# First loads on three queues, memory chunks scaled on two engines, the last row stored in four pieces, and another instruction order

## Chip, cores and metric

One core of a Trainium2 chip runs the kernel as one launch. Its engines are TensorE (PE, matrix products; PEld is its loading of weights), VectorE (DVE), ScalarE (ACT), GpSimd (POOL) and SyncE (SP). SP, ACT and POOL issue DMA transfers, each on a queue of its own. The metric is the device time of one execution in microseconds (us), as the median of several runs.

## What is computed

A decoder block over 512 positions of width 1024 (D), with 256 memory tokens, four heads of 256, and a feed-forward width of 2816:

```python
h = rmsnorm(x); proj = h @ w_in                      # 9216 columns
p_a, p_b, q, p_g = split(proj)
y_a = (gb * causal_conv3(gc * v)) @ w_a_out          # gb, gc, v from p_a
y_b = silu(layernorm(causal_conv31(u * sigmoid(ug)) + bias)) @ w_b_out
k, vm = split((rmsnorm(mem) * norm_mem_g) @ w_kv)
y_c = attention(q, k, vm) @ w_att_out
x = x + (g0 * y_a + g1 * y_b + g2 * y_c) @ w_o       # g = sigmoid(p_g + b_gate)
u = causal_conv3(rmsnorm(x) @ w_up); gt, up = split(u)
x = x + (silu(gt) * up) @ w_down
return rmsnorm(x) * norm_final_g
```

Inputs, weights and output are 32-bit floats.

## The kernel before

**Products.** A 32-bit matrix is split into a high part (rounded to the type that PE multiplies fast) and a low part (the rest). `product` (L632 to L636) makes three matmuls of each: high times high, high times low, low times high. ACT forms the high part of a weight block by a cast (`whi`, L683), DVE the low part by a subtraction (`wlo`, L687). Weights arrive in blocks of 512 KB (128 x 1024).

**Quads.** The big projections are cut into quads of 512 output channels, multiplied with seven products in place of eight: products 1 to 7 of a quad use sums and differences of blocks of the weights and of the activations (`ft4` to `ft7`, `fb00`, `fb10`, `fb11`). Sums of weights are made by adding transfers on POOL's queue (L808) or on DVE. One product is `multiply` (L866): 24 matmuls with 256 columns. Several products share a PSUM bank, and between them somebody must read the bank: product 4 may start only when DVE has read product 7's result with `minus` (L640, tile `uu`), products 6 and 7 after reads by ACT, and so on. A first matmul of a product is written with another access pattern of the same data (128x2x8x16 in place of 128x256) where the table `FRESH` names it.

**The order.** The kernel describes its work as jobs, each with an engine, a cost, the jobs it follows and the buffers it takes. A planner (`Jobs`) works out a due time for each from the order on PE and sets every engine's order. Three tables move its choices: `LATER` shifts due times, `AHEAD` tells how early a job may be issued, and `MOVES` edits the order on PE. The instructions are then written to the program in this order, so each engine runs through a fixed list.

**The start.** PE runs 11 warm-up products (`warm_up`, L2105) on a constant. SP loads the first half of the memory (`mem`, L947), then K's first weights (`ld0 K`, L1081), then V's; ACT's queue loads the gains (`pk`, 128 x 16, L628). When both are there ACT scales the four chunks of the memory by their gains (`mg`, L954), and PE multiplies the keys' first tile straight from these (K0, L1146), in two halves that wait for two chunks each. ACT then makes the memory's high part (`mh`, L966), DVE its low part (`ml`, L977), for the products after it.

**The end.** The output has four row tiles (t = 0 to 3) of 128 positions. For the last one DVE adds the two last banks (L2429), ACT sums squares (L2432) and takes the root (L2453), DVE the reciprocal (L2501). Then DVE scales the left 512 columns (`left_scaled`, L2463) and ACT the right ones (`right_scaled`, L2459), and SP and ACT each store a half (`stored`, L2468).

Of the kernel before, what the change touches and what calls it, by code (L numbers as in the profile page):

```python
# [8 lines left out]
F32 = mybir.dt.float32  # L9
F32R = mybir.dt.float32r  # L10
AF = mybir.ActivationFunctionType
# [3 lines left out]
P = 128  # L15
# [62 lines left out]
    "ACT c3": -190.4, "ACT cf": 13.1, "ACT csq": 651, "ACT exp": -246.7, "ACT fh h b00": -1,  # L78
# [4 lines left out]
    "ACT mg0": 6, "ACT mgh a": 11.9, "ACT mgh b": -6, "ACT mgh c": -22.7, "ACT mgh d": -539,  # L83
    "ACT mgh e": -123, "ACT mgh g": 4, "ACT mh": 472, "ACT mu high": 22, "ACT oh": -68.6,
    "ACT pth": -80, "ACT qh": -60.7, "ACT r1 bb": 75, "ACT r1 cv": 61.8, "ACT r1 gate": 335.4,
# [5 lines left out]
    "ACT sc": -95, "ACT sg": -4.8, "ACT sigmoid": 49, "ACT silu": 91, "ACT sq": -65, "ACT sr": -14,  # L91
    "ACT st": -0.2, "ACT swish": -944, "ACT tap 0": 323, "ACT tap 1": 95, "ACT tap 2": 5,
# [8 lines left out]
    "ACT xg": 33.2, "ACT xroot": -347, "ACT xsquare": 120, "ACT zh a": -186, "ACT zh b": -50,  # L101
    "ACT zh c": -3.4, "ACT zh e": -11, "ACT zh f": -93, "ACT zh g": -0.8, "DVE CV": 16.7,
    "DVE c3": -233, "DVE centre": 100, "DVE cf": 121.1, "DVE csum": -12, "DVE ends": -93.7,
# [6 lines left out]
    "DVE lns": -4.6, "DVE low": -427, "DVE m scale": -18, "DVE mfold": 2, "DVE mfold2": 277,  # L110
    "DVE mgl a": -2.1, "DVE mgl b": -5, "DVE mgl c": -11, "DVE mgl d": 400.7, "DVE mgl g": -334.1,
    "DVE ml": 82, "DVE ms c": -232, "DVE ms e": -2.2, "DVE ms f": 266, "DVE msum": -7,
    "DVE mu fold": -70, "DVE mu low": -150, "DVE mu sum": -187, "DVE ol": 10.7, "DVE pn": -22.2,
# [7 lines left out]
    "DVE sum": 167.8, "DVE tap 0": 898, "DVE tap 1": 336, "DVE tap 2": 0.8, "DVE tap 3": 567,  # L121
    "DVE top": -3576.1, "DVE tot1": 143.2, "DVE tot2": -268.9, "DVE v scale": 78.8,
    "DVE var fold": 114, "DVE var sum": 8, "DVE vl": -9.8, "DVE weigh": -226, "DVE wl K 0": 89.1,
# [8 lines left out]
    "DVE xn": 12.6, "DVE xnorm": -40, "DVE xsum": 40.6, "DVE y t4": -169, "DVE y t5": -5,  # L132
# [9 lines left out]
    "POOL wadd x": -1269, "POOL wadd y": 4, "POOL wl merge 0": 3.3, "POOL wl merge 2": -163.8,  # L142
# [372 lines left out]
def hybrid_block_kernel(  # L515
# [429 lines left out]
    for g in range(2):  # L945
# [1639 lines left out]
```

## Time and profile before

| what | value |
|---|---|
| runs, without the profiler | 918.60, 918.65, 918.81 us; median 918.65 us |
| profiled execution, its own time | 918.8 us |
| its span, first to last instruction | 917.0 us |
| granted TensorE clock, mean | 0.999 of full speed |
| PE busy / DVE / ACT / POOL | 908.5 / 848.7 / 684.6 / 137.1 us |
| transfers | 196.91 MB, mean 215 GB/s |

In a list of waits a row names the waiting engine, its tile and line, then the engine that ended the wait, and after the colon the total in us, the number of waits and the longest one. A row of the timeline has the start in us, the duration, the engine, the line, the operation, the tile it writes and those it reads, a count, and in brackets the idle time ahead of it with what ended it. SPq and ACTq are transfers as issued by these engines. A row that ends in KB and a number tells the median time in us from a transfer's issue to its landing. A row of the stretches has the window, its length, and for each engine its busy time and instructions, then PE's clock, the transfers' share and their GB/s; with one engine asked for, only that one.

### The profile page before, as it was taken

What the parts mean: (1) busy time and instruction counts of PE and PEld (TensorE: products, weight loads), DVE (VectorE), ACT (ScalarE), POOL (GpSimd) and SP (SyncE); (2) the same over time, 40 slices, a digit from 0 to 9 for tenths busy, and PEclk for the clock granted to TensorE, in tenths of its full rate; (3) what the DMA queues carried; (4) which work ended last, traced back from release to release, by engine and by line L of the source; (5) the groups of instructions that cost most, each with busy time, mean ns of one, the idle gap of its engine ahead of it and who ended that gap; (6) DMA issues with size and microseconds to landing.
All of it is one profiled execution on the core that took longest, in us unless ns stands there. A gap on an engine that the chain in (4) does not pass through costs nothing.

```text
span 917.0 us, 17020 instructions
## 1 busy us (share of the span) xinstructions
PE 908.5 (99%) x6789; PEld 858.7 (94%) x6789; DVE 848.7 (93%) x965; ACT 684.6 (75%) x940; POOL 137.1 (15%) x164
## 2 busy tenths in 40 slices
PE   9999999999999999999999999999999999999997
PEld 8999999999989999999899997899999999988886
DVE  6996999999999999999898989898979899999977
ACT  7777978889988876879748874767757676765566
POOL 0021111101011121110111211121211111002210
PEclk9999999999999999999999999999999999999999
DMA  9999778746769799786958999999999687779962
GB/s 367 371 293 196 153 177 201 157 117 150 212 144 274 167 197 239 151 185 176 227 126 242 204 260 322 260 219 293 276 259 215 143 194 161 191 258 316 270 136 93
DMA packets 55377, 196.91 MB, mean 215 GB/s; under 512 B 6273, under 2 KB 6401, under 8 KB 55297
## 3 DMA queue, kind: packets, MB, share of 16 engines
q0 software_dynamic: 22608, 81.54, 49.4%
q1 hardware_dynamic: 32400, 114.02, 34.3%
q8 instruction: 53, 0.87, 0.4%
q10 hardware_dynamic: 288, 0.27, 0.1%
q14 instruction: 28, 0.22, 0.1%
HBM read 191.60 MB, written 4.19 MB: 214 GB/s over the span
## 4 chain that ended last, share of the span: by engine, by line
PE 99%; DVE 1%; issue 0%; ACT 0%; DVEq 0%
PE bank L866 65%; PE bank L634 7%; PE bank L636 7%; PE bank L635 7%; PE bank L1705 3%; PE bank L1706 3%; PE bank L1704 3%; PE bank L1157 2%; PE bank L1938 1%; PE bank L2105 1%; PE bank L1146 0%; PE bank L1400 0%; PE bank L1993 0%; PE ss L1021 0%; DVE z L2073 0%
## 5 line engine op out<-in xcount | busy, mean ns | idle before, releaser
L683 ACT CAST whi<-wf 128x1024 fp32r<-128x1024 f32 (+1 forms) x197 | 205.2, 1044 | 96.4 <-PE bank L866 48.7
L687 DVE TENSOR_TENSOR wlo<-wf,whi 128x1024 fp32r<-128x1024 f32 (+1 forms) x191 | 230.0, 1213 | 12.3 <-ACT whi L683 12.0
L1472 ACT ACTIVATE tp<-u,pk 128x511 f32<-128x511 f32 (+22 forms) x184 | 119.0, 705 | 6.9 <-DVE acc L1479 5.8
L1479 DVE TENSOR_TENSOR acc<-acc,tp 128x1022 f32<-128x1022 f32 (+22 forms) x92 | 109.4, 1191 | 8.4 <-ACT tp L1472 6.8
L808 POOL DMA_DIRECT2D wf<-in_w_in x43 | 39.4, 938 | 217.0 <-DVE wlo L687 187.2
L866 PE MATMUL bank<-ft4h,whi 128*128 128x256 f32 x248 | 68.6, 277 | 0.9 <-DVE uu L640 0.9
L866 PE MATMUL bank<-fb10h,whi 128*128 128x256 f32 x248 | 68.7, 277 | 0.0
L866 PE MATMUL bank<-fb00h,whi 128*128 128x256 f32 x248 | 68.7, 277 | 0.0
L866 PE MATMUL bank<-ft7h,whi 128*128 128x256 f32 x248 | 68.7, 277 | 0.0
L866 PE MATMUL bank<-ft5l,whi 128*128 128x256 f32 x248 | 68.7, 277 | 0.0
L866 PE MATMUL bank<-fb11h,whi 128*128 128x256 f32 x248 | 68.7, 277 | 0.0
L866 PE MATMUL bank<-ft6l,whi 128*128 128x256 f32 x248 | 68.6, 277 | 0.0
L866 PE MATMUL bank<-ft6h,whi 128*128 128x256 f32 x248 | 68.6, 277 | 0.0
L866 PE MATMUL bank<-ft6h,wlo 128*128 128x256 f32 x248 | 68.6, 276 | 0.0
L866 PE MATMUL bank<-ft7l,whi 128*128 128x256 f32 x248 | 68.6, 276 | 0.0
L866 PE MATMUL bank<-ft5h,whi 128*128 128x256 f32 x248 | 68.6, 276 | 0.0
L866 PE MATMUL bank<-ft5h,wlo 128*128 128x256 f32 x248 | 68.5, 276 | 0.0
L866 PE MATMUL bank<-ft7h,wlo 128*128 128x256 f32 x248 | 68.5, 276 | 0.0
L866 PE MATMUL bank<-fb10l,whi 128*128 128x256 f32 x248 | 68.5, 276 | 0.0
L866 PE MATMUL bank<-fb10h,wlo 128*128 128x256 f32 x248 | 68.5, 276 | 0.0
L866 PE MATMUL bank<-ft4l,whi 128*128 128x256 f32 x248 | 68.5, 276 | 0.0
L866 PE MATMUL bank<-fb00l,whi 128*128 128x256 f32 x248 | 68.5, 276 | 0.0
(418 smaller groups left out, 3172.1 us busy)
## 6 DMA issues: line engine op xcount, KB each, us to landing
wf<-in_w_in SPq DMA_DIRECT2D x50, 512.0 KB, 5.9
wf<-in_w_in POOLq DMA_DIRECT2D x43, 512.0 KB, 6.6
wf<-in_w_up SPq DMA_DIRECT2D x31, 512.0 KB, 6.9
wf<-in_w_up POOLq DMA_DIRECT2D x30, 512.0 KB, 7.2
wf<-in_w_down SPq DMA_DIRECT2D x15, 512.0 KB, 6.1
wf<-in_w_kv SPq DMA_DIRECT2D x8, 512.0 KB, 8.7
wf<-in_w_v SPq DMA_DIRECT2D x8, 512.0 KB, 8.1
wf<-in_w_att_out SPq DMA_DIRECT2D x8, 512.0 KB, 4.1
```

Of the source, the lines that this page charges most:

```text
L634: nc.tensor.matmul(ps, s_hi, w_hi, start=start, stop=False, skip_group_check=again)
L635: nc.tensor.matmul(ps, s_hi, w_lo, start=False, stop=False, skip_group_check=again)
L636: nc.tensor.matmul(ps, s_lo, w_hi, start=False, stop=stop, skip_group_check=again)
L683: nc.scalar.copy(parts[0], src())
L687: nc.vector.tensor_tensor(lo, src(), hi.bitcast(F32), op=ALU.subtract)
L808: nc.gpsimd.dma_start(out=tiles[key], in_=block(w, col[c], k), accum_op=ALU.add)
L866: nc.tensor.matmul(to, w[:, k, at], col, start=first and n == 0, stop=k == 3 and n == 2, skip_group_check=again,)
L1472: nc.scalar.activation(two(("tp", p, s))[:, j, s:], two(("u", p))[:, j, : SEQ - s], AF.Copy, scale=weight(j),)
L1479: nc.vector.tensor_tensor(a, a, two(("tp", p, s))[:, :, s:], op=ALU.add)
L1704: nc.tensor.matmul(ps, w_hi[:, i, at], hi, start=first, stop=False)
L1705: nc.tensor.matmul(ps, w_hi[:, i, at], lo, start=False, stop=False)
L1706: nc.tensor.matmul(ps, w_lo[:, i, at], hi, start=False, stop=last)
```

## The change

Five edits:

1. The load of the gains goes to POOL's queue, ahead of POOL's first work; the constant `mean_w` is made by DVE in place of ACT.
2. K's first weights are loaded from ACT's queue in place of SP's.
3. The four memory chunks are scaled on ACT (chunks 0 and 2) and DVE (1 and 3) in place of ACT alone, as four jobs.
4. Both halves of the last row are scaled in two pieces of 256 columns (`ENDS`), and each piece is stored by itself: the left two from SP, the right first one from POOL, the right second one from ACT.
5. `LATER`, `AHEAD`, `FRESH` and some of `MOVES` have other entries.

```diff
 LATER = {
-    "ACT c3": -190.4, "ACT cf": 13.1, "ACT csq": 651, "ACT exp": -246.7, "ACT fh h b00": -1,
...
+    "ACT cf": 470, "ACT exp": -1067.2, "ACT fh h b00": -451, "ACT fh h b10": -0.1,
...
 FRESH = {
-    (("glu", 2), 7), (("q", 1), 5), (("bb", 0), 7), (("bb", 1), 1), (("gate", 0, 1), 2),
-    (("up", 2), 1), (("up", 0), 5), (("up", 0), 4), (("up", 1), 4), (("up", 2), 6),
+    (("glu", 2), 7), (("q", 1), 5), (("q", 1), 7), (("cv", 0), 7), (("cv", 2), 1), (("bb", 1), 2),
+    (("gate", 0, 0), 4), (("mq", 1), 3), (("up", 0), 5), (("up", 0), 6), (("up", 0), 4),
+    (("up", 1), 7), (("up", 1), 4), (("up", 2), 6),
 }
 MOVES = [
...
-    ((("up", 1), 7), (("up", 1), 4)),
-    ((("up", 1), 2), (("up", 0), 5)),
-    (("tr", 0), ("tr", 1)),
+    (("tr", 2), ("tr", 3)),
+    (("tr", 0), ("wo", "g", 0, 1)),
...
 AHEAD = {
...
+    pk = const.tile([P, N_PACKED], F32, tag="pk", name="pk")
+    nc.gpsimd.dma_start(out=pk[:, :N_GAINS], in_=packed[:, :N_GAINS])
     make_identity(nc, ident)
...
     nc.vector.memset(mean_col, 1.0 / D)
+    nc.vector.tensor_copy(mean_w, mean_col.broadcast_to([P, P]))
     nc.scalar.preload_act_table_set("sqrt_and_others")
-    nc.scalar.dma_start(out=pk[:, :N_GAINS], in_=packed[:, :N_GAINS])
-    nc.scalar.copy(mean_w, mean_col.broadcast_to([P, P]))
...
-            def mem_scaled(e=e):
-                if e == 0:
-                    make(("mg0",))
-                for i in range(2 * e, 2 * e + 2):
-                    nc.scalar.activation(
-                        four(("mg0",))[:, i, :], four(("mem", 0))[:, i, :], AF.Copy,
-                        scale=par("norm_mem_g", i),
-                    )
+            def mem_scaled(i):
+                to, t, scale = four(("mg0",))[:, i, :], four(("mem", 0))[:, i, :], par("norm_mem_g", i)
+                if i % 2:
+                    nc.vector.tensor_scalar(to, t, scale, None, op0=ALU.mult)
+                else:
+                    nc.scalar.activation(to, t, AF.Copy, scale=scale)
...
-        job(("ld0", s), "SP", LOAD, lambda: nc.sync.dma_start(out=tiles[raw], in_=src),
-            [("raw tile", s)], LOAD_LATENCY, use=[raw])
+        job(("ld0", s), "SP", LOAD, lambda: (nc.scalar if s == "K" else nc.sync).dma_start(
+            out=tiles[raw], in_=src), [("raw tile", s)], LOAD_LATENCY, use=[raw])
...
-                   lambda e=e: keys_product(0, 0, (2 * e, 2 * e + 1)), [("ld0", "K"), ("mg0", e)],
+                   lambda e=e: keys_product(0, 0, (2 * e, 2 * e + 1)), [("ld0", "K"), ("mg0", 2 * e), ("mg0", 2 * e + 1)],
...
+        for e, part in enumerate(ENDS if t == last else (slice(0, SEQ),)):
+            job(("sl", t, e), "DVE", 0.37 if t == last else 0.67,
+                lambda t=t, part=part: left_scaled(t, part), [("rc", t)])
+            job(("st", t, 0, e), "SP", STORE, lambda t=t, part=part: stored(t, 0, nc.sync, part),
+                [("sl", t, e)], LOAD_LATENCY)
+        for e, part in enumerate(ENDS if t == last else (slice(0, SEQ),)):
+            job(("sc", t, e), "ACT", 0.4 if t == last else 0.62,
+                lambda t=t, part=part: right_scaled(t, part),
+                [("rc", t), ("hd", t)] + ([("sc", t, 0)] if e else []))
+            queue, on, cost = ("SP", nc.sync, STORE)
+            if t == last:
+                queue, on, cost = (("ACT", nc.scalar, 0.4) if e else ("POOL", nc.gpsimd, 0.9))
+            job(("st", t, 1, e), queue, cost, lambda t=t, part=part, on=on: stored(t, 1, on, part),
+                [("sc", t, e)], LOAD_LATENCY)
```

**The order at the start.** ACT's first rows (each row: line, operation, the tile written and those read, its size) before, and in the changed program. `wf` with `in_w_kv` is K's first weights, `whi` the high part of V's.

```order
L627 ACT_TABLE_LOAD
L628 DMA pk<-in_packed 128x16
L629 CAST mean_w<-mean_col 128x128
L954 ACTIVATE mg_8_118<-mem_95,pk 128x256 x4
L966 CAST mh_129<-mg_8_118 128x512 x2
L1091 CAST whi_141<-wf_97 128x512 x2
```

```order
L626 ACT_TABLE_LOAD
L1080 DMA wf_96<-in_w_kv 128x1024
L952 ACTIVATE mg_6_112<-mem_95,pk 128x256 x2
L961 CAST mh_123<-mg_6_112 128x512 x2
L1090 CAST whi_141<-wf_97 128x512 x2
```

ACT now issues K's load in place of the gains, and scales two chunks in place of four; SP's list goes from `mem` straight to V's first weights.

**The order around product 7 of quad up 1.** PE before and after. `bank_6975` before and `bank_6959` after are the same bank of that quad; `ft7` and `ft4` are the operands of its products 7 and 4, `ft5` that of product 5 of quad up 2 (`bank_7414`).

```order
L866 MATMUL bank_6975<-ft7h_7101,whi_7333 128x256
L866 MATMUL bank_6975<-ft7l_7102,whi_7333 128x256
L866 MATMUL bank_6975<-ft7h_7101,wlo_7334 128x256
L866 MATMUL bank_6975<-ft4h_7207,whi_7372 128x2x8x16
L866 MATMUL bank_6975<-ft4l_7208,whi_7372 128x256
```

```order
L863 MATMUL bank_6959<-ft7h_7101,whi_7300 128x256
L863 MATMUL bank_6959<-ft7l_7102,whi_7300 128x256
L863 MATMUL bank_6959<-ft7h_7101,wlo_7301 128x256
L863 MATMUL bank_7414<-ft5h_7067,whi_7334 128x256
L863 MATMUL bank_7414<-ft5l_7068,whi_7334 128x256
L863 MATMUL bank_7414<-ft5h_7067,wlo_7335 128x256
```

Before, product 4 follows product 7 of its quad directly; now the 24 matmuls of product 5 of the next quad stand between them.

**The order at the end.** ACT's last rows before, and in the changed program. `x_1236` is the last row tile, `j` the squares' scratch, `cols` the sums.

```order
L2459 ACTIVATE x_1235_9730<-x_1235_9730,cols 128x512
L2432 ACTIVATE j_9646,cols<-x_1236_9731 128x256 x2
L2453 ACTIVATE cols<-cols 128x1
L2459 ACTIVATE x_1236_9731<-x_1236_9731,cols 128x512
L2468 DMA out<-x_1236_9731 128x512
```

```order
L2458 ACTIVATE x_1235_9729<-x_1235_9729,cols 128x512
L2431 ACTIVATE j_9646,cols<-x_1236_9730 128x256 x2
L2452 ACTIVATE cols<-cols 128x1
L2458 ACTIVATE x_1236_9730<-x_1236_9730,cols 128x256 x2
L2467 DMA out<-x_1236_9730 128x256
```

The scaling is now two instructions, and ACT stores one quarter of the row; POOL's list now ends with such a store too, and SP's with two.

More of the change, by code (lines that the diff above doesn't have):

```diff
@@ new lines @@
+    "ACT fh y t7": -2.4, "ACT high": -4.2, "ACT kh": 6.5, "ACT m root": -60, "ACT mg0": -13,
+    "ACT mgh a": 624, "ACT mgh b": -3, "ACT mgh c": 139.8, "ACT mgh d": 224.7, "ACT mgh g": 231,
+    "ACT mh": 238, "ACT msq": -372.8, "ACT mu high": 79, "ACT pth": -99.7, "ACT r1 bb": -395.5,
[6 rows of a table added]
+    "ACT sigmoid": -2.6, "ACT silu": -186, "ACT sq": -48, "ACT sr": -39, "ACT st": -158,
+    "ACT swish": -889.5, "ACT tap 0": 10.9, "ACT tap 1": 196.2, "ACT tap 2": -200.5,
[9 rows of a table added]
+    "ACT xg": 33.4, "ACT xroot": -141, "ACT xsq": 3.3, "ACT xsquare": -21, "ACT zh a": -322,
@@ new lines @@
+    "ACT zh b": -124.5, "ACT zh c": 17, "ACT zh d": 156, "ACT zh e": 118.3, "ACT zh g": 15.1,
+    "DVE CV": 8.9, "DVE c3": -2535, "DVE centre": 11.5, "DVE cf": 383, "DVE csum": -3,
[6 rows of a table added]
+    "DVE kt": 361.5, "DVE lns": -3.2, "DVE low": -120, "DVE m scale": 194, "DVE mfold": 187,
+    "DVE mfold2": -359.7, "DVE mgl a": 35, "DVE mgl b": 3.6, "DVE mgl c": -235.7, "DVE mgl d": 26.2,
+    "DVE mgl e": -35.6, "DVE mgl g": -1.4, "DVE ml": 3, "DVE ms c": -181.7, "DVE ms d": -47.9,
+    "DVE ms f": -1138, "DVE msum": 836, "DVE mu fold": -484, "DVE mu low": -59.2, "DVE mu sum": 208,
@@ new lines @@
+    "DVE ol": -602, "DVE pn": -694, "DVE ptl": -2738, "DVE ql": -793, "DVE r2 bb": -27,
[6 rows of a table added]
+    "DVE sum": 661.9, "DVE tap 0": 163, "DVE tap 2": -31.6, "DVE tap 3": 1414.3, "DVE top": -2751.7,
+    "DVE tot1": 118, "DVE tot2": 107, "DVE um": 329.9, "DVE v scale": -8, "DVE var sum": -40,
[8 rows of a table added]
+    "DVE x1 g": -263, "DVE xfold": -58.6, "DVE xn": -10, "DVE xnorm": -138.3, "DVE y t4": 79.5,
[8 rows of a table added]
+    "POOL s7 gate": -102, "POOL s7 glu": -189, "POOL s7 up": -73, "POOL wadd e": -208,
+    "POOL wadd x": -280, "POOL wadd y": 2.8, "POOL wl merge 0": -113, "POOL wl merge 2": 4.1,
[6 rows of a table added]
@@ L173 @@
     ((("up", 5), 7), (("up", 7), 1)),
[L174 to L186 removed]
+    ((("up", 5), 6), (("up", 7), 5)),
+    ((("up", 4), 3), (("up", 5), 6)),
+    ((("up", 4), 4), (("up", 4), 3)),
+    ((("up", 5), 2), (("up", 4), 4)),
+    ((("up", 3), 3), (("up", 6), 1)),
+    ((("up", 4), 7), (("up", 6), 5)),
+    ((("up", 3), 4), (("up", 4), 7)),
+    ((("up", 4), 6), (("up", 5), 1)),
+    ((("up", 3), 7), (("up", 4), 6)),
+    ((("up", 3), 6), (("up", 4), 2)),
+    (("tr", 2), ("tr", 3)),
+    (("tr", 0), ("wo", "g", 0, 1)),
     ((("mq", 1), 2), (("mq", 1), 6)),
@@ L236 @@
 AHEAD = {
[3 rows of a table removed]
-    "ACT high": 10, "ACT kh": 20, "ACT m root": 5, "ACT mgh c": 10, "ACT mgh d": 40,
-    "ACT mgh g": 10, "ACT mh": 5, "ACT oh": 2, "ACT pth": 20, "ACT qh": 2, "ACT r1 bb": 80,
[4 rows of a table removed]
-    "ACT swish": 150, "ACT tap 3": 80, "ACT tp 3": 150, "ACT v root": 150, "ACT vh": 80,
[4 rows of a table removed]
-    "ACT xsq": 80, "ACT xsquare": 150, "ACT zh a": 80, "ACT zh b": 40, "ACT zh c": 10,
[3 rows of a table removed]
-    "DVE h2 t4": 40, "DVE hd": 40, "DVE low": 150, "DVE m scale": 10, "DVE mfold": 20,
-    "DVE mgl a": 10, "DVE mgl b": 5, "DVE mgl c": 150, "DVE mgl e": 40, "DVE ml": 150,
-    "DVE ms d": 20, "DVE ms e": 10, "DVE msum": 150, "DVE mu fold": 2, "DVE mu low": 2,
-    "DVE mu sum": 20, "DVE ol": 10, "DVE pn": 5, "DVE ptl": 10, "DVE ql": 40, "DVE r2 bb": 20,
[4 rows of a table removed]
-    "DVE sl": 20, "DVE tap 2": 150, "DVE top": 20, "DVE tot1": 150, "DVE tot2": 10,
-    "DVE var sum": 20, "DVE vl": 10, "DVE wl K 0": 150, "DVE wl merge 2": 5, "DVE wl mix 3": 5,
[9 rows of a table removed]
-    "POOL wadd x": 20, "POOL wadd y": 40, "POOL wl merge 0": 10, "POOL wl merge 2": 2,
[4 rows of a table removed]
+    "ACT csq": 10, "ACT fh h b10": 5, "ACT fh h t4": 150, "ACT fh h t5": 20, "ACT fh h t6": 20,
+    "ACT fh h t7": 80, "ACT fh h2 t4": 10, "ACT fh h2 t5": 150, "ACT fh h2 t7": 150,
+    "ACT fh y b00": 10, "ACT high": 5, "ACT kh": 20, "ACT m root": 20, "ACT mg0": 20,
+    "ACT mgh b": 5, "ACT mgh e": 20, "ACT msq": 20, "ACT oh": 10, "ACT pth": 150, "ACT r1 bb": 40,
[3 rows of a table added]
+    "ACT st": 150, "ACT swish": 80, "ACT tap 3": 40, "ACT tp 2": 150, "ACT tp 3": 150,
[4 rows of a table added]
+    "ACT wn merge 2": 40, "ACT wn wo 0": 80, "ACT x root": 5, "ACT xg": 40, "ACT xroot": 5,
+    "ACT xsq": 80, "ACT xsquare": 10, "ACT zh c": 150, "ACT zh e": 150, "ACT zh f": 40,
+    "ACT zh g": 20, "DVE CV": 150, "DVE c3": 10, "DVE centre": 20, "DVE csum": 40,
[3 rows of a table added]
+    "DVE low": 40, "DVE mfold2": 5, "DVE mgl a": 80, "DVE mgl b": 10, "DVE mgl c": 2,
+    "DVE mgl d": 40, "DVE mgl e": 150, "DVE mgl g": 2, "DVE ml": 20, "DVE ms c": 2, "DVE ms d": 150,
+    "DVE ms e": 10, "DVE ms f": 150, "DVE mu low": 10, "DVE ol": 2, "DVE pn": 2, "DVE ptl": 150,
[4 rows of a table added]
+    "DVE top": 10, "DVE tot1": 150, "DVE tot2": 150, "DVE v scale": 20, "DVE var fold": 20,
[4 rows of a table added]
+    "DVE x1 d": 80, "DVE x1 e": 2, "DVE x1 f": 150, "DVE xfold": 80, "DVE xsum": 2, "DVE ymul": 40,
[8 rows of a table added]
 }
@@ L990, in hybrid_block_kernel @@
             if g == 0:
-                job(("mg0", e), "ACT", 2 * scaled_act(256), mem_scaled,
-                    [("mg0", 0) if e else ("ldm", 0, 0)],
-                    take=[] if e else [(source, ANY)], use=[("mem", 0)] + ([source] if e else []))
-            ready = ([] if e else [("ldm", 1, 0)]) if g else [("mg0", e)]
+                if e == 0:
+                    job(("mg0 tile", 0), "NONE", 0.0, lambda: make(("mg0",)), [("mem tile", 0)],
+                        take=[(source, ANY)])
+                for i in (2 * e, 2 * e + 1):
+                    job(("mg0", i), "DVE" if i % 2 else "ACT", 0.36 if i % 2 else scaled_act(256),
+                        lambda i=i: mem_scaled(i), [("ldm", 0, 0), ("mg0 tile", 0)],
+                        use=[("mem", 0), source])
+            ready = ([] if e else [("ldm", 1, 0)]) if g else [("mg0", 2 * e), ("mg0", 2 * e + 1)]
             job(("mh", g, e), "ACT", 2 * scaled_act(256) if g else actv(512), mem_high,
@@ L2127, in hybrid_block_kernel @@
         for side in sides
-    } | {("mg0", e) for e in range(2)}
+    } | {("mg0", i) for i in range(4)}
     GLU = [("glu", p) for p in range(4)]
@@ L2455, in root, with right_scaled, left_scaled, stored @@
         )
-    def right_scaled(t):
-        x1 = late["x1"][t][1]
+    def right_scaled(t, cols=slice(0, SEQ)):
+        x1 = late["x1"][t][1][:, cols]
         nc.scalar.activation(x1, x1, AF.Copy, scale=r_fin[t])
-    def left_scaled(t):
-        x1 = late["x1"][t][0]
+    def left_scaled(t, cols=slice(0, SEQ)):
+        x1 = late["x1"][t][0][:, cols]
         nc.vector.scalar_tensor_tensor(
-            x1, x1, r_fin[t], late["g"][0], op0=ALU.mult, op1=ALU.mult
+            x1, x1, r_fin[t], late["g"][0][:, cols], op0=ALU.mult, op1=ALU.mult
         )
-    def stored(t, i, queue):
+    def stored(t, i, queue, cols=slice(0, SEQ)):
         queue.dma_start(
-            out=out[t * P : (t + 1) * P, i * 512 : (i + 1) * 512], in_=late["x1"][t][i]
+            out=out[t * P : (t + 1) * P, i * 512 + cols.start : i * 512 + cols.stop],
+            in_=late["x1"][t][i][:, cols],
         )
```

38 lines of the change are left out of this document (1 added, 37 removed), and 162 rows, old and new, of tables (AHEAD, LATER).

## The prediction

> **What bounds the kernel now.** I read the page's first part, then the chain of waits, then what TensorE (PE) waits for, then the span cut into stretches.
>
> ```profile
> span 917.0 us, 17020 instructions
> PE 908.5 (99%) x6789; PEld 858.7 (94%) x6789; DVE 848.7 (93%) x965; ACT 684.6 (75%) x940; POOL 137.1 (15%) x164
> PE 99%; DVE 1%; issue 0%; ACT 0%; DVEq 0%
> PE bank L2105 <- DVE mean_col L626: 0.9, 1, 0.9
> PE bank L866 <- DVE uu L640: 0.9, 1, 0.9
> PE bank L636 <- DVE zl L2274: 0.4, 1, 0.4
> 6.00:300.00 294.00, 294.00 (x2230) 280.00 (x2230) 276.60 (x321) 247.16 (x366) 40.00 (x46) 1.00 0.82 217
> 910.70:917.00 6.30, 0.00 (x0) 0.00 (x0) 1.41 (x4) 1.52 (x4) 0.00 (x0) 0.82 0.57 218
> ```
>
> PE is busy 908.5 of 917.0 us. The chain agrees, and the list of PE's waits (total, count, mean) says how little there is to win inside: 0.9 at the start, one wait of 0.9 for the vector engine's (DVE's) `uu`, one of 0.4 for its `zl`. The stretch 6 to 300 us has PE busy 294.00 of 294.00, and the last 6.30 us hold no matmul. As the change leaves every product in place, it can touch four things only: when the first real product starts, the waits in the middle, waits that the new order makes, and the tail. What lies outside the span is 918.8 − 917.0 = 1.8 us and I leave it alone. The profiled 918.8 is 0.15 over the median 918.65, to which I add the sum.
>
> **The start.** Rows of the queues and engines in order of time, then issue to landing:
>
> ```profile
> 0.74 0.39 SPq L947 DMA_DIRECT2D mem<-in_mem_t  x1
> 1.19 0.42 SPq L1081 DMA_DIRECT2D wf<-in_w_kv  x1
> 1.66 0.42 SPq L1081 DMA_DIRECT2D wf<-in_w_v  x1
> 0.77 0.39 ACTq L628 DMA_DIRECT2D pk<-in_packed  x1
> mem<-in_mem_t SPq DMA_DIRECT2D x1, 512.0 KB, 3.9
> wf<-in_w_kv SPq DMA_DIRECT2D x1, 512.0 KB, 4.7
> pk<-in_packed ACTq DMA_DIRECT2D x1, 8.0 KB, 4.0
> 4.90 1.71 ACT L954 ACTIVATE mg<-mem,pk 128x256 f32<-128x256 f32 x4 [2.57 <-DMA pk<-in_packed]
> 0.93 5.06 PE L2105 MATMUL bank<-mean_col 128*128 128x128 f32 x22 [0.93 <-DVE mean_col L626]
> 5.98 4.08 PE L1146 MATMUL bank<-mg,wf 128*128 128x256 f32 x16
> ```
>
> Landings: mem 0.74 + 3.9 = 4.64, pk 0.77 + 4.0 = 4.77, K's weights 1.19 + 4.7 = 5.89. The scaling starts at 4.90, 0.13 after pk. The first K product starts at 5.98, when three things have come together: the weights (5.89), two scaled chunks (4.90 + 1.71 / 2 = 5.76), and PE itself, whose warm-up runs to 0.93 + 5.06 = 5.99. The warm-up is not changed, so an earlier landing or a faster scaling wins nothing here: the lower bound of this term is 0. This is the first expected gain that is hidden anyway.
>
> What can be lost: K's load now leaves ACT's queue beside mem's on SP, instead of behind it. That queues share the engines is seen in pk: 8 KB took 4.0 us beside a load of 512 KB that took 3.9. Two loads of 512 KB issued together should then end together, at the time when both were in before, 5.89. Then the chunks start at 5.89 + 0.13 = 6.02. A pair, one chunk on ACT beside one on DVE, takes 1.71 / 4 = 0.43, and 0.1 more to the product: 6.6 instead of 5.98, **+0.6**.
>
> A rule speaks against this part. The Trainium skill, DMA: Bandwidth & Descriptors, section "Rules for kernel authors", says that spreading loads over SP, ACT and GpSimd brings no bandwidth, because all run on the same 16 engines and interleave; it saves issue time only. The trace agrees with its 4.0 beside 3.9. By this rule the term is a loss or nothing, never a gain.
>
> The other price is pk on POOL's queue, whose first load it is. Nearest rows, POOL quiet and POOL's first load of the old order, beside a lone load on SP and POOL's usual one:
>
> ```profile
> wf<-in_w_in POOLq DMA_DIRECT2D x1, 512.0 KB, 5.6
> ('glu', 0)_60_362<-in_w_in POOLq DMA_DIRECT2D x1, 512.0 KB, 9.5
> wf<-in_w_a_out SPq DMA_DIRECT2D x8, 512.0 KB, 3.8
> wf<-in_w_in POOLq DMA_DIRECT2D x43, 512.0 KB, 6.6
> ```
>
> These POOL loads add to their target, which pk does not, so they bound from above. A quiet POOL costs 5.6 − 3.8 = 1.8 more than SP: pk would land at 0.77 + 4.0 + 1.8 = 6.57, and the first product start at about 7.25, +1.3. The first one took 9.5, and with that whole time pk lands at 10.3 and the product starts at 11.0, +5.0. The lower end is no surcharge, when mem's 5.89 decides. I take +0.6 because 8 KB need a small part of what 512 KB need. Bounds of the term: 0 to +5.0. What follows has cover: V's load leaves SP at K's old place and is still the third half megabyte. The copy of `mean_w` on DVE is free, DVE being idle until mem's scaling.
>
> **The wait of 0.9.** PE's rows around it, and DVE's:
>
> ```profile
> 634.35 0.28 PE L866 MATMUL bank<-ft7h,wlo 128*128 128x256 f32 x1
> 635.49 0.39 PE L866 MATMUL bank<-ft4h,whi 128*128 128x256 f32 x1 [0.86 <-DVE uu L640]
> 634.74 0.69 DVE L640 SCALAR_TENSOR_TENSOR uu<-bank,uu 128x512 f32<-128x512 f32 x1 [0.33 <-PE bank L866]
> ```
>
> Product 7 of quad up 1 ends at 634.63, DVE reads its bank for 0.69, and product 4, whose bank that is, waits. This is a loop PE → DVE → PE with no work between. In the new order product 5 of up 2 stands between; ten of these matmuls at 0.28 cover more than 0.69, and it has 24. So the wait goes with its lengthened first matmul: 0.86 + (0.39 − 0.28) = 0.97, **−0.95**. Lower bound of the gain 0, if product 5 finds another late operand.
>
> **The wait of 0.4** comes out of a race of DVE with PE (a stretch: length, busy; then rows):
>
> ```profile
> 771.94:824.60 52.66, 52.38 (x60) 1.00 0.73 218
> 771.94 0.69 DVE L900 TENSOR_TENSOR gt<-gt,bank 128x512 f32<-128x512 f32 x1 [0.48 <-PE bank L866]
> 824.66 0.50 PE L636 MATMUL bank<-whi,zl 128*128 128x512 f32 x1 [0.37 <-DVE zl L2274]
> 680.94 1.23 DVE L687 TENSOR_TENSOR wlo<-('up', 4)_977_7479,whi 128x1024 fp32r<-128x1024 f32 x1 [2.04 <-ACT whi L683]
> ```
>
> From 771.94, where PE released it, to 824.60 DVE is busy 52.38 of 52.66 us, and then PE waits for its last result. The new order holds the same DVE work ahead of that `zl`, only shuffled, so I leave this wait: **0**, bounds −0.4 to +2.0. The upper end is what a gap like the 2.04 at 680.94 would cost if it fell into this stretch.
>
> **New waits.** Order differences on PE touch about 20 of its 355 pieces of work, on DVE and ACT over half, so some read of a bank or some low part may now be late. The whole old order has 0.9 + 0.4 = 1.3 us of such waits. I take a quarter, **+0.3**, since each bank still has a whole product between its read and its next use; bounds 0 to +1.3.
>
> **The end.**
>
> ```profile
> 910.40 0.28 PE L636 MATMUL bank<-whi,zl 128*128 128x256 f32 x1
> 910.71 0.42 DVE L2429 TENSOR_TENSOR x<-x,bank 128x256 f32<-128x256 f32 x1 [0.32 <-PE bank L636]
> 912.03 0.17 DVE L2501 RECIPROCAL cols<-cols 128x1 f32<-128x1 f32 x1 [0.83 <-ACT cols L2453]
> 912.23 0.75 DVE L2463 SCALAR_TENSOR_TENSOR x<-x,cols,gfin 128x512 f32<-128x512 f32 x1
> 912.23 0.72 ACT L2459 ACTIVATE x<-x,cols 128x512 f32<-128x512 f32 x1 [0.23 <-DVE cols L2501]
> 912.99 0.38 ACTq L2468 DMA_DIRECT2D out<-x  x1
> out<-x ACTq DMA_DIRECT2D x1, 256.0 KB, 2.8
> out<-x SPq DMA_DIRECT2D x1, 256.0 KB, 2.6
> out<-x SPq DMA_DIRECT2D x7, 256.0 KB, 2.2
> ```
>
> Both halves are ready at 912.98; the stores land at 912.99 + 2.8 = 915.8 and slightly before. Up to 912.23 nothing changes. Then a piece of 256 columns costs DVE 0.42 (the row at 910.71) and ACT 0.43, so pieces are ready at 912.65 and 913.1; the second ones are 0.1 later than now. They leave on SP and ACT with less beside them, at the usual 2.2: 913.15 + 2.2 = 915.35, a gain of 0.45. The right first piece leaves POOL at 912.7: with 2.2 it lands at 914.9, with the whole POOL surcharge of 1.8 at 916.7, +0.9. With half of it 915.8, less a little because the piece is half as large: 915.7, **−0.1**, bounds −0.45 to +0.9.
>
> **Sum:** +0.6 − 0.95 + 0 + 0.3 − 0.1 = −0.15 us: 918.65 − 0.15 = **918.5**.
>
> **The rivals.**
> A, slower: pk through POOL is late and the whole program starts behind it. For it: it is POOL's first load and everything hangs on these gains; against it: 8 KB only. If it pays what the first load paid over the usual one, 9.5 − 6.6 = 2.9, it lands at 0.77 + 4.0 + 2.9 = 7.67, and the product starts at 8.35: +2.4 in place of +0.6, 920.3; with the far end 922.9. It decides from a landing after 5.89 on, and ends over 0.2% from about 7.9.
> B, slower: the shuffled DVE stretch gets a gap because a high part from ACT comes late. For it: gaps of 2.04 exist shortly before it and DVE has 0.28 us of air in 52.66; against it: ACT is busy only 75%. Any gap over about 0.1 there is PE's: −0.15 + 2.04, 920.55.
> C, the better side: mem is served first, pk is early and the start stays at 5.98; POOL's piece is not the last. 0 − 0.95 + 0 − 0.45 + 0 = −1.4: 917.25, and 916.85 if the `zl` wait goes too. For it: ACT issues K after SP has issued mem; against it: pk's 4.0. The Trainium skill, DMA: Bandwidth & Descriptors, section "Queues, rings and completion order", says that an engine takes turns between queues by whole packets of some 9 to 17 descriptors. With 128 rows over 16 engines, 8 each, mem would then go as one, and C's time would follow; no run here shows which.
> D, the reorder does not do what it says: the 0.97 stays or is handed to the `zl` wait, since a PE that arrives earlier waits longer for the same DVE. For it: that race; against it: between 635 and 771.94 DVE is released by PE again. −0.15 + 0.95: 919.45.
>
> **How the numbers follow.** The forecast gets 0.5, A 0.14, B 0.14, C 0.15, D 0.07. The forecast's own range is 917.5 to 919.6. 0.2% is 1.84 us, about what a measurement of this kernel can tell from no change: the bounds are 916.81 and 920.49. Faster: 0.04 of the forecast, 0.07 of C, 0.02 of D's opposite (PE's waits all gone): 0.13. Slower: 0.08 of A, 0.09 of B, 0.03 of the forecast: 0.20. The rest is 0.67. The range 916.5 to 921.0 leaves out A's far half (0.07), some of B (0.03) and 0.05 below.
>
> **What would show it.** The first K product at 6.6, with mem and K landing together near 5.9 and pk not after them: at 5.98 C holds, past 7.5 A. No wait for `uu` after product 7 of up 1, and PE's waits in the middle together about 0.7. DVE without a gap before the first `zl` that PE waits for; a gap with PE waiting there is B. Last stores landing between 4.6 and 5.0 us after the last matmul's end at 910.68 of the old clock, with POOL's piece among the last. Wrong altogether I would be if PE's busy time itself moved by more than 1 us from 908.5.

## The result, and the profile after

The changed kernel took 920.98 us, the median of 11 runs, against 918.79 for the kernel before in the same comparison: a ratio of 1.0027, 95% interval 1.0019 to 1.0036, slower. The forecast was 918.5 and no change. The profiled execution, 923.75 with a span of 922.0, is the longest of these runs; a second profile of the same kernel, shown below as after_again, is nearer the median with a span of 919.4.

The page's first lines and the list of PE's waits, of the changed kernel:

```profile
span 922.0 us, 17055 instructions
PE 909.6 (99%) x6789; PEld 859.5 (93%) x6789; DVE 849.3 (92%) x969; ACT 684.3 (74%) x938; POOL 138.7 (15%) x166
PE bank L1145 <- ACT mg L952: 1.5, 1, 1.5
PE bank L863 <- ACT whi L680: 1.3, 1, 1.3
PE bank L2104 <- DVE mean_col L624: 0.9, 1, 0.9
PE bank L863 <- ACT gt L890: 0.4, 1, 0.4
PE bank L633 <- DVE zl L2273: 0.2, 1, 0.2
```

The wait for `uu` is gone and the one for `zl` is down from 0.4 to 0.2. New are 1.5 for the scaled chunks at the start, 1.3 for a weight block's high part, and 0.4 for a read `gt`. The 1.3 begins at a late transfer, for which ACT waited before it made four high parts in a row:

```profile
622.47 3.89 ACT L680 CAST whi<-wf 128x1024 fp32r<-128x1024 f32 x4 [3.25 <-DMA wf<-in_w_up]
```

The start, in the changed kernel's transfers (issue to landing) and its engines' rows:

```profile
mem<-in_mem_t SPq DMA_DIRECT2D x1, 512.0 KB, 5.1
wf<-in_w_kv ACTq DMA_DIRECT2D x1, 512.0 KB, 5.3
pk<-in_packed POOLq DMA_DIRECT2D x1, 8.0 KB, 5.6
1.29 0.70 POOL L612 DMA_DIRECT2D pk<-in_packed  x1 [0.84 <-POOLq L2577]
6.92 0.91 ACT L952 ACTIVATE mg<-mem,pk 128x256 f32<-128x256 f32 x2 [4.89 <-DMA pk<-in_packed]
7.48 3.72 PE L1145 MATMUL bank<-mg,wf 128*128 128x256 f32 x16 [1.49 <-ACT mg L952]
```

mem lands at 0.75 + 5.1 = 5.85 and K's weights at 0.78 + 5.3 = 6.1, the forecast's 5.89 for both. But the 8 KB of gains, issued by POOL at 1.29, land at 6.9, after both, and ACT starts right then. The first K product starts at 7.48 instead of 5.98.

The end, in the timeline, the landings, and the view of the program's last line (durations in ns: least, median, most; then first and last start):

```profile
916.21 0.57 POOL L2467 DMA_DIRECT2D out<-x  x1 [40.89 <-ACT x L2458]
out<-x POOLq DMA_DIRECT2D x1, 128.0 KB, 2.8
out<-x ACTq DMA_DIRECT2D x1, 128.0 KB, 2.0
L2586 POOLq DRAIN  x3: 51/93/5009, 916.2 to 921.7; - x3
L2586 SPq DRAIN  x3: 7/7/7, 919.6 to 921.5; - x3
```

POOL's store has landed at 916.21 + 2.8 = 919.0. SP is through with its own waits at 919.6. Then everybody waits for POOL: its drain, the wait at the end of POOL's list, starts with its store at 916.2 and takes 5.0 us, to 921.2, which is 2.2 after the store's landing. The kernel before has a long drain too, but early:

```profile
872.15 2.63 POOL L2339 DMA_DIRECT2D y_sum<-in_w_down  x1
y_sum<-in_w_down POOLq DMA_DIRECT2D x1, 256.0 KB, 15.9
L2581 POOLq DRAIN  x3: 45/102/18231, 871.9 to 916.8; - x3
```

There POOL's last transfer is a load issued at 872.15, which lands 15.9 later, at 888.0. The drain runs from 871.9 for 18.2 us, to 890.2, 2.1 after that landing, and is over 27 us before the end. The two short ones, 0.05 and 0.10 us, stand at the very end.

### The profile page after: what moved, and what is told of

The parts are those of the page before. It is cut to its first block, busy times and chain, and to the rows that moved or that the text cites. A ratio compares the mean times of both kernels' runs of the same rounds, so it can differ in the third digit from the quotient of the medians.

```text
span 922.0 us, 17055 instructions
## 1 busy us (share of the span) xinstructions
PE 909.6 (99%) x6789; PEld 859.5 (93%) x6789; DVE 849.3 (92%) x969; ACT 684.3 (74%) x938; POOL 138.7 (15%) x166
## 4 chain that ended last, share of the span: by engine, by line
PE 82%; issue 6%; DVE 5%; DMA 4%; ACT 2%; SPq 1%; POOLq 0%; ACTq 0%; DVEq 0%
PE bank L863 60%; PE bank L1704 3%; PE bank L1705 3%; PE bank L1703 3%; PE bank L631 3%; PE bank L633 3%; PE bank L632 3%; PE bank L1156 2%; DVE wlo L684 2%; DMA wf<-in_w_down 1%; DMA wf<-in_w_up 1%; DMA x_sum<-in_w_down 1%; DVE zl L2273 1%; PE bank L1937 1%; ACT whi L680 1%
## 5 line engine op out<-in xcount | busy, mean ns | idle before, releaser
L1478 DVE TENSOR_TENSOR acc<-acc,tp 128x1018 f32<-128x1018 f32 (+22 forms) x92 | 109.1, 1188 | 6.5 <-ACT tp L1471 4.7
L863 PE MATMUL bank<-fb00h,wlo 128*128 128x256 f32 x248 | 68.6, 277 | 0.0
L863 PE MATMUL bank<-ft4h,wlo 128*128 128x256 f32 x248 | 68.6, 276 | 0.0
```

Source lines behind the costliest of these rows:

```text
L863: nc.tensor.matmul(to, w[:, k, at], col, start=first and n == 0, stop=k == 3 and n == 2, skip_group_check=again,)
L1478: nc.vector.tensor_tensor(a, a, two(("tp", p, s))[:, :, s:], op=ALU.add)
```

## The experiments

Each is timed against the kernel before on the same chip, on three chips in all; its median in those comparisons lay between 918.2 and 918.8, and each difference below is taken within its own comparison. In the first four the order on PE is exactly that of the kernel whose tables they have, so the parts come apart cleanly.

**start_only**: edits 1 to 3 (first loads, chunks on two engines).

```diff
+    nc.gpsimd.dma_start(out=pk[:, :N_GAINS], in_=packed[:, :N_GAINS])
...
-        job(("ld0", s), "SP", LOAD, lambda: nc.sync.dma_start(out=tiles[raw], in_=src),
+        job(("ld0", s), "SP", LOAD, lambda: (nc.scalar if s == "K" else nc.sync).dma_start(
...
+                if i % 2:
+                    nc.vector.tensor_scalar(to, t, scale, None, op0=ALU.mult)
```

> The kernel before with edits 1 to 3 alone (gains from POOL's queue, K's load from ACT's, chunks on two engines), old tables, old end. Theory: the whole program follows the late first K product. It starts at about 7.5 us instead of 5.98 because the gains land at 6.9, the product itself runs some 0.3 shorter, so the time is about 1.1 to 1.2 us above the kernel before, a ratio near 1.0012, and the three old waits of PE stay in place. Rival, forecast on record: K's load beside mem's costs the +0.6 and the gains are not late. Rival, hidden: the late start is made up by smaller waits at the two places where PE waits for DVE (0.9 and 0.4), so the ratio is within 0.0005 of 1.

Measured: 921.38, ratio 1.0026 (1.0014 to 1.0038), runs from 919.43 to 924.32. The start alone costs 2.6 us, as much as the whole change, and 1 us more than its late first product explains. The profile says where the rest is; PE's rows, and PE by stretches (window, length, busy time and count, granted clock, transfers):

```profile
0.93 4.26 PE L2107 MATMUL bank<-mean_col 128*128 128x128 f32 x22 [0.93 <-DVE mean_col L627]
7.57 5.41 PE L1148 MATMUL bank<-mg,wf 128*128 128x256 f32 x16 [2.38 <-ACT mg L955]
4.00:6.00 2.00, 1.19 (x10) 1.00 1.03 419
6.00:8.00 2.00, 0.43 (x1) 0.90 1.03 418
8.00:10.00 2.00, 2.00 (x6) 0.50 1.03 424
10.00:12.00 2.00, 2.00 (x9) 0.75 1.02 418
```

The warm-up is over at 5.19 and PE stands still for 2.38 us. Then the granted clock falls to 0.5, and the K product takes 5.41 us; at full clock it took 3.72 in the changed kernel. So this execution, whose span is 3.1 longer than before, pays 1.6 for the late start and 1.7 for the clock.

**end_only**: edit 4 (four pieces, one from POOL).

```diff
+            queue, on, cost = ("SP", nc.sync, STORE)
+            if t == last:
+                queue, on, cost = (("ACT", nc.scalar, 0.4) if e else ("POOL", nc.gpsimd, 0.9))
```

> The kernel before with edit 4 alone (the last row in four pieces, one stored from POOL), old tables, old start. Theory: the landings are not what sets the end; POOL's own drain after its transfer is, 5.0 us from 916.2 in the changed kernel's profile. Span from the last matmul's end to the end about 8.1 instead of 6.3, +1.8 us or a ratio near 1.0020. Rival: the long drain belongs to the profiled execution only, since its time was 2.8 above the median; then the tail is about the landing plus 1.2, and the ratio between 0.9995 and 1.0010.

Measured: 919.71, ratio 1.0011 (1.0002 to 1.0019). POOL's drain is there again, from 912.1 to 917.05 of a span of 917.8, and again ends 2.2 after the landing of POOL's store (914.9):

```profile
L2587 POOLq DRAIN  x3: 51/93/4937, 912.1 to 917.5; - x3
```

So the drain belongs to the kernel and not to one execution; the rival's ground is gone. In this profile the last matmul ends at 909.8 and the span 8.0 later, where it was 6.3: +1.7, as the theory has it. The loss in the median is only +0.9, with an interval of 0.2 to 1.7 us.

**order_only**: edit 5 (the tables).

```diff
 LATER = {
-    "ACT c3": -190.4, "ACT cf": 13.1, "ACT csq": 651, "ACT exp": -246.7, "ACT fh h b00": -1,
+    "ACT cf": 470, "ACT exp": -1067.2, "ACT fh h b00": -451, "ACT fh h b10": -0.1,
...
-    ((("up", 1), 7), (("up", 1), 4)),
```

> The kernel before with edit 5 alone (tables), old start and old end. Theory from the two traces: the wait of 0.9 for uu is gone, a wait of 1.3 for a weight block's high part in quad up 0 and one of 0.4 in quad up 1 have come, and a stretch of 45 us in which matmuls follow each other at 0.118 instead of 0.113 us, together some +1 to +2 us over the kernel before. Rival, forecast on record: the order by itself gains 0.65 us, and what the profiled execution showed near 625 was a late transfer of that one execution, so the ratio is about 0.9993.

Measured: 917.54, ratio 0.9985 (0.9976 to 0.9994). The theory of a loss is refuted, the forecast on record held in direction: the new order is faster by 1.3 us (0.5 to 2.2). Its waits:

```profile
PE bank L1143 <- DMA wf<-in_w_kv: 0.9, 1, 0.9
PE bank L863 <- ACT gt L890: 0.4, 1, 0.4
```

No `uu`, no `zl`, no 1.3 near 625. The 0.9 for `wf` is no loss against before: the warm-up was over sooner here, and the product began at 5.94.

The waits alone do not explain the gain. From the start of the K product to the start of the last matmul, the three profiles of the new order with PE at its usual pace (order_only, order_and_end_two, after_again) take 903.2 to 903.4 us. The old order, with the clock at 1.0, takes 903.4 in end_two and in end_only, although both waits, 0.9 and 0.4, are there in full, and 904.0 to 904.8 in before, base_again, pool_row2, start_k_sp and start_warm. So against the old order's best profiles the new one wins nothing over this stretch. What differs is the spread: order_only's runs lie between 917.25 and 917.81, the compared runs of the kernel before between 917.70 and 921.06. What makes the old order's longer executions longer is only in part in the lists (waits for `gt` of 0.3 to 0.9 in three of these five), and the rest stays open.

**after_again**: the changed kernel, a second profile.

> The changed kernel once more, for a second profile. If the 5.0 us drain of POOL and the wait of 1.3 near 625 are properties of the kernel they are there again; the first profile took 923.75, 2.8 over the median of its runs, so at least one of the drain, the wait, or the slow stretch behind it should be smaller this time. The first K product is expected at 7.5 again.

Measured: 921.77, ratio 1.0034 (1.0021 to 1.0048); the profiled execution took 921.19.

```profile
PE bank L1145 <- ACT mg L952: 1.6, 1, 1.6
PE bank L863 <- ACT gt L890: 0.4, 1, 0.4
L2586 POOLq DRAIN  x3: 51/93/4994, 913.6 to 919.1; - x3
```

The late start and the drain came again, to 0.2 us. The 1.3 near 625 did not: the late transfer belongs to the first profile's execution. The parts add up within their intervals, each about 1 us to either side: +2.6 (start), +0.9 (end), −1.3 (order) make +2.2, and 920.98 − 918.79 is 2.2; in this second comparison the changed kernel is 3.0 slower.

**start_pk_act**: the start edits with the gains on ACT's queue, ahead of K's load.

```diff
     nc.scalar.preload_act_table_set("sqrt_and_others")
+    nc.scalar.dma_start(out=pk[:, :N_GAINS], in_=packed[:, :N_GAINS])
```

> The start edits with the gains back on ACT's queue, ahead of K's load there; K's load stays on ACT's queue beside mem's on SP. Theory P (the gains on POOL's queue are the loss): the gains land near 5 us, mem and K's weights share the engines and land together at 5.3 to 6.1, the first K product starts at 6.2 to 6.6, and the median is +0.3 to +0.7 over the kernel before (start_only was +2.6). Theory S (the sharing is the loss, and the gains were late only because two large loads ran beside them): the gains land with mem near 6 or later, the product starts at 6.9 or later, and the median stays at +1.5 or more.

Measured: 921.88, ratio 1.0035 (1.0022 to 1.0047).

```profile
mem<-in_mem_t SPq DMA_DIRECT2D x1, 512.0 KB, 3.8
wf<-in_w_kv ACTq DMA_DIRECT2D x1, 512.0 KB, 6.2
pk<-in_packed ACTq DMA_DIRECT2D x1, 8.0 KB, 4.0
7.55 5.38 PE L1148 MATMUL bank<-mg,wf 128*128 128x256 f32 x16 [1.95 <-ACT whi L1093]
```

Neither theory. The gains land at 4.8 and mem at 4.6, as before the change. But K's weights, issued on ACT's queue at 1.19, now land at 7.4 in place of 5.9: V's first load stands on SP's queue behind mem alone, is issued at 1.18, and lands at 6.8, ahead of K. The product starts at 7.55 for this other reason. The row names a cast of ACT's, but K's landing at 7.4 is what the product needs and what came last. It takes 5.38, as in start_only, and the clock again reads 0.50 for 3.41 us, from 8.46 to 11.87.

**start_k_sp**: the start edits with K's load back on SP.

```diff
-        job(("ld0", s), "SP", LOAD, lambda: (nc.scalar if s == "K" else nc.sync).dma_start(
+        job(("ld0", s), "SP", LOAD, lambda: nc.sync.dma_start(
```

> The start edits with K's load back on SP, second there; only the gains are on POOL's queue. Theory P: mem lands at 4.6 as before, but the gains still need about 5.7 us from their issue at 1.29 and land at 7.0; the product starts at 7.5 and the median stays near start_only's 921.4. Theory S: with one large queue beside them the gains land at about 5.3 (1.29 + 4.0), the product starts near 5.95, and the median is within 0.3 of the kernel before.

Measured: 918.91, ratio 1.0007 (0.9998 to 1.0016): not to be told from no change.

```profile
mem<-in_mem_t SPq DMA_DIRECT2D x1, 512.0 KB, 3.7
wf<-in_w_kv SPq DMA_DIRECT2D x1, 512.0 KB, 4.5
pk<-in_packed POOLq DMA_DIRECT2D x1, 8.0 KB, 4.6
6.43 3.72 PE L1148 MATMUL bank<-mg,wf 128*128 128x256 f32 x16 [1.29 <-ACT mg L955]
```

Theory P is refuted, and S is near: with one large queue beside them the gains from POOL take 4.6 (S had 4.0) and land at 5.9, with two they take 5.6 to 5.8 and land at 6.9 to 7.1. The loss of the start is K's load on a queue of its own: start_only, start_pk_act and start_warm, which have it, lose 1.8 to 3.3 us. Without it, with the gains on POOL's queue and the chunks on two engines, the product starts 0.45 later and the median is 0.4 up, which the interval does not tell from nothing.

**start_warm**: start_only with a longer warm-up.

```diff
-        for i in range(11):
+        for i in range(16):
```

> start_only with 16 warm-up products in place of 11. Theory C (clock): in start_only the time beyond the late start came from PE standing still between warm-up and first product for 1.5 to 2.4 us, after which the granted clock fell to 0.5 for 3.4 us in some executions (its profile: 7.6 to 11.0) and the product took 5.4 in place of 3.7. With PE busy until 6.3 to 7.6 it stays at full clock: runs lie within about 1 us of each other, where start_only's spread over 4.9, and the median comes down from 921.4 to 919.6 to 920.3. Rival L: the spread comes from transfers later in the program; then five more products change nothing, or add what the warm-up runs past 7.5.

Measured: 920.35, ratio 1.0022 (1.0012 to 1.0032), runs from 919.53 to 922.19. The first product starts at 7.53 and takes 3.72, at full clock. The median is 1.8 over its kernel before, where start_only's was 2.6 over, but the two intervals overlap, so the medians alone show no gain. The granted clock, averaged over each run, does show what changed: it is 0.998 or 0.999 in all eight runs, as in the compared runs of the kernel before, and 0.996 or 0.997 in six of start_only's twelve. So the clock is part of the start's loss. The spread is 2.7 in place of 4.9, not the 1 that theory C wanted; the rest of it has another cause, and this profile shows a wait of 0.9 for a read `gt` that in the old order's other profiles is absent or up to 0.6.

**base_again**: the kernel before, a second profile.

> The kernel before once more, for a second profile. Its own spread shows how much of a difference a single profile can show: first K product between 5.9 and 6.1, the three waits of 0.9 at 635, 0.4 at 825 present, last matmul's end between 909.7 and 910.7, 6.3 us from there to the end, ratio 1 within 0.0005.

Measured: 918.75, ratio 1.0000 (0.9991 to 1.0008). The first product starts at 6.01, the waits for `uu` and `zl` are 0.9 and 0.4 again, and there is a wait of 0.3 for a read `gt`: this one is not the new order's own. The warm-up took 4.78 here and 5.06 in the first profile.

**end_two**: four pieces at the end, none from POOL.

```diff
-                queue, on, cost = (("ACT", nc.scalar, 0.4) if e else ("POOL", nc.gpsimd, 0.9))
+                queue, on, cost = (("ACT", nc.scalar, 0.4) if e else ("SP", nc.sync, STORE))
```

> The kernel before with the last row in four pieces, none of them stored from POOL: three from SP, one from ACT. Theory D (POOL's drain is the loss of the end): no long drain, from the last matmul's end to the end of the span 5.9 to 6.3 us (7.9 to 8.2 with POOL's piece), median at or up to 0.3 under the kernel before. Rival: four small stores cost as much by themselves, three of them issued one after another; then the tail stays above 6.8 and the ratio near end_only's 1.0011.

Measured: 918.26, ratio 0.9997 (0.9988 to 1.0006). POOL's long drain runs from 870.3 to 890.0, as in the kernel before, and the span ends 6.1 us after the last matmul (909.6 to 915.7), against 8.0 with POOL's piece. Theory D holds. The four pieces by themselves gain 0.2 of the 6.3 in this profile, and nothing in the median that can be told from no change.

**pool_row2**: two halves at the end as before, but the third row's right half is stored from POOL.

```diff
-            job(("st", t, 1), "SP", STORE, lambda t=t: stored(t, 1, nc.sync), [("sc", t)],
-                LOAD_LATENCY)
+            job(("st", t, 1), "POOL" if t == 2 else "SP", STORE, lambda t=t: stored(
+                t, 1, nc.gpsimd if t == 2 else nc.sync), [("sc", t)], LOAD_LATENCY)
```

> The kernel before with the right half of the third row stored from POOL in place of SP; it is ready about 2 us before the last row's halves. Theory D1 (the drain takes 5.0 us from POOL's last transfer, whatever else runs): the drain runs from about 910.2 to 915.2 and is over before the last stores land at 915.8, so the tail stays at 6.3 and the median within 0.2 of the kernel before. Theory D2 (the drain ends a fixed time after all stores): the tail grows to about 8 again, ratio 1.0010 or more.

Measured: 918.54, ratio 0.9996 (0.9987 to 1.0005).

```profile
L2581 POOLq DRAIN  x3: 51/102/5029, 910.7 to 917.1; - x3
910.77 0.58 POOL L2468 DMA_DIRECT2D out<-x  x1 [32.02 <-ACT x L2459]
```

The drain is as long, 5.03 us, but starts at 910.7, is over at 915.8, before SP is done at 916.5, and costs nothing that can be told: the tail is 6.4. D2 is refuted: the drain does not wait for the other engines' stores. D1 is right in that it goes by POOL's last transfer, but 5.0 us is not its length in general: the store landed at 913.6, and the drain ended 2.2 after it. In the 14 profiles it ends 2.1 to 2.2 us after the landing of POOL's last transfer, whether it lasts 5 us or, with the loads of the kernel before, 18.

**move_only**: the old tables without one entry.

```diff
 MOVES = [
...
-    ((("up", 1), 7), (("up", 1), 4)),
```

> The kernel before without the one entry of MOVES that puts product 7 of quad up 1 right ahead of its product 4. Forecast's term: the wait of 0.9 for uu near 635 goes and nothing takes its place, median 0.95 under the kernel before, near 917.6 to 917.8, ratio 0.9990. Rival: the wait is given back at 825, where DVE's last zl decides, or at another read near 640; then PE's waits sum to the old 1.3 us and the ratio is 0.9995 to 1.0003.

Measured: 925.12, ratio 1.0069 (1.0055 to 1.0082), outside all that was expected. The wait for `uu` is gone, but another has come; its waits, ACT's rows ahead of it, and PE by stretches:

```profile
PE bank L865 <- ACT gt L892: 3.6, 1, 3.6
PE bank L865 <- DVE wlo L686: 0.9, 2, 0.7
637.57 0.60 ACT L915 ACTIVATE uu<-bank 128x512 f32<-128x512 f32 x1 [3.95 <-PE bank L865]
639.13 1.28 ACT L2089 ACT_TABLE_LOAD   x1
640.43 1.06 ACT L2089 ACTIVATE gtc<-gtc 128x1024 f32<-128x1024 f32 x1
641.39 1.03 ACT L682 CAST whi<-('up', 3)_965_7370 128x1024 fp32r<-128x1024 f32 x1
642.33 1.04 ACT L682 CAST whi<-wf 128x1024 fp32r<-128x1024 f32 x1
643.27 0.58 ACT L892 COPY gt<-bank 128x512 f32<-128x512 f32 x1
640.00:645.00 5.00, 0.76 (x5) 1.00 1.08 280
645.00:650.00 5.00, 4.93 (x28) 0.66 1.04 267
```

The planner answered the one entry with other places for its neighbours, over a dozen each on ACT and DVE. ACT now stands 3.95 us waiting for a bank of PE's, and only then come a read, a cast, the table load, the activation, two casts and the read of `gt` that releases product 6. PE waits 3.6 us for it, then 0.7 for a low part, and the granted clock falls on top, to a mean of 0.66 over the next five us. The term "635 wait goes" is real, but belongs to the whole set of tables, not to this entry.

**order_and_end_two**: the new tables, four pieces without POOL, the old start.

> The new tables with the old start, and the last row in four pieces without POOL. If the parts add, order_only's -1.25 and end_two's 0 to -0.3: 917.2 to 917.5, ratio 0.9982 to 0.9986, faster than both kernels. If end pieces cost, 918.

Measured: 917.44, ratio 0.9986 (0.9976 to 0.9996): faster than the kernel before by what order_only gains alone, and so faster than the changed kernel too.

## Why the prediction was wrong, step by step

**What bounds the kernel**: right. PE's busy time is 909.6 in the first profile of the changed kernel and 908.2 in the second, against 908.5. The 1.1 of the first passes the 1 us that the forecast named as a sign of being wrong altogether; it comes from the slower pace of that one execution (last section). The third number in the list of waits is the longest, not the mean; for single waits the two are the same. The differences are PE's late start, its waits, its pace and the tail.

**The start** ("+0.6"): the step that failed. Two loads on two queues did land together, at 5.85 and 6.1, as reckoned. The error is in the sentence that takes +0.6 "because 8 KB need a small part of what 512 KB need". Small as they are, the gains are served last, at 6.9, and the start moves by +1.5 instead of +0.6. The row that hinted at it was in the fence: 8 KB took 4.0 beside one full queue, as long as its 512 KB; beside two full queues they take 5.6, again as long as the large loads. It is rival A's outcome with a smaller delay than A's 7.67, but not A's cause: A put it on POOL's first load, and with the gains on POOL's queue and K back on SP's they land at 5.9 and the loss is 0.4. The second part of the loss was not in the forecast at all: the pause ahead of the product is long enough for the clock to fall in some executions, at 1.7 us in start_only's profile. The start was reckoned at 0.6 and measured at 2.6.

The Trainium skill's rule on spreading loads (DMA: Bandwidth & Descriptors, "Rules for kernel authors") was the better guide: no bandwidth was won (265 GB/s over the first 7.6 us, against 270 before), and mem and the gains, which are needed first, were slowed by what ran beside them. Another rule of the Trainium skill, that whole packets are served in turn (same page, "Queues, rings and completion order"), gave rival C, in which mem lands as before: with K issued at the same time mem took 5.1 to 5.3 instead of 3.9, so that did not happen; with K issued 0.45 later (start_pk_act) mem took 3.8. The profile counts a packet of such a load as one row of 4 KB (8 packets with 0.03 MB in the first 1.9 us), so mem was not one packet an engine, as C had it.

"The warm-up runs to 5.99" was true of that execution only. It ended at 5.0 to 6.0 in others, and the first product started at 5.9 to 6.1 all the same, since K's weights land then. The bound of no gain stands for the weights' sake.

**The wait of 0.9** ("−0.95"): right, the wait is absent in every profile with the new order. Its cover was mis-sized: matmuls of 0.28 overlap, and 24 of them take 2.7 us and not 6.7; the margin over DVE's 0.69 was still enough. **The wait of 0.4** ("0"): it is 0.2 or gone, a gain of 0.2 to 0.4. **New waits** ("+0.3"): 0.4 for `gt`, which the old order has too in some executions. In sum the order gave −1.3 in the median where these terms had −0.65, but not by the waits alone, as order_only shows.

**The end** ("−0.1", bounds −0.45 to +0.9): the transfers behaved nearly as reckoned, POOL's store landing in 2.8 where 2.2 plus half of 1.8 was taken, and 5.1 us after the last matmul's end where 4.6 to 5.0 was named. What failed is the step from landing to end, which was taken as the old 1.2. The end is set by POOL's drain, which ends 2.2 after its store lands: +0.9 in the median, +1.7 in end_only's tail. The profile before could have shown it: there POOL's drain ends at 890.2, 2.1 after its last load landed at 888.0. Put behind the forecast's own landing at 915.7, with the 0.8 that pass between SP's first drain (916.2) and the end of the span (917.0), that makes an estimate of 918.6 and a term of +1.6.

**The range** 916.5 to 921.0 holds 920.98 by its edge only, and that is luck: the start and the end lost 3.0 more than reckoned, and the order gave 0.65 more, without which the time would lie near 921.6. The likeliest case was the wrong one: 0.67 stood on no change, 0.20 on slower.

## What to carry to other kernels

In these runs a load that was needed first came later when another large load started beside it on a second queue, so put on other queues only what may come later. A few KB were no exception: 3.9 to 4.6 us beside one full queue, 5.6 to 5.8 beside two. Look at what POOL's last transfer is and when it lands: here its drain ended 2.1 to 2.2 us after that, so a store of POOL's at the very end made the kernel longer, and one issued 2.5 us earlier did not. And after a warm-up a pause of two microseconds can cost more than its length: look at the granted clock behind every wait that a change creates.

## What the runs showed of the hardware

**The clock falls to half for 3.41 us.** In start_only it was 0.5 from 7.6 to 11.0, 3.41 us, after a pause of 2.38; in start_pk_act from 8.46 to 11.87, after one of 1.95; in move_only from 645.08 to 648.49, after the wait of 3.6. With pauses of 1.3 (start_k_sp) and 1.5 to 1.6 (both profiles of the changed kernel) it stayed at 1.0. The Trainium skill (TensorE: Matmul & The Clock Gate, Part 1) tells of a window of about 3.4 us that runs free of the program; the 3.41 agree. That only some of start_only's runs have a low mean clock fits a window that runs free. The section speaks of an idle window; here a pause of 2.0 to 2.4 us was enough.

**A slower pace without a lower clock.** In the first profile of the changed kernel PE by stretches reads:

```profile
655.00:665.00 10.00, 10.00 (x87) 1.00 1.06 271
670.00:680.00 10.00, 10.00 (x87) 1.00 1.04 233
690.00:700.00 10.00, 10.00 (x91) 1.00 0.82 185
```

From a wait at 642.6 until about 688, 87 matmuls took the 10 us of 90 or 91, at a granted clock of 1.00: some 1.7 us. With the 1.3 near 625 that is 3.0; the span is 2.6 longer than after_again's, which had lost some 0.6 of its own earlier. There the same wait was followed by the usual pace:

```profile
655.00:665.00 10.00, 10.00 (x91) 1.00 1.05 257
670.00:680.00 10.00, 10.00 (x90) 1.00 1.06 230
```

Why the pace falls in one execution and not in the next, and what ends it, was not tried and stays open.
